# Seven-product weight blocks: low parts by adding transfers in place of VectorE subtractions

## The chip, the cores and the metric

One Trainium2 chip, one core. The metric is the device time of one execution in microseconds (us). The kernel before took 2408.53 us, the median of three runs (2404.02, 2408.53 and 2409.84).

## What is computed

One layer of a decoder trunk on a sequence of 1024 tokens with 1024 channels, all in float32. The part that this case touches is the wide dense products:

```python
u = x * (1.0 + scale1) + shift1
hq, hf, hi, hg, rq, rk, rv, rg, ga, gb = jnp.split(u @ w_in[l], split_at, axis=-1)
...
u = x * (1.0 + scale2) + shift2
h = jnp.square(jax.nn.relu(u @ w_up[l] + b_up[l]))
y = h @ w_down[l] + b_down[l]
```

Between them stand two recurrences (a gated linear one with 8 heads and a retention with 4), their output projections, and two LayerNorms. They stay as they are.

## The kernel before

**Three matmuls for one.** A float32 product is made of three passes in a rounded float32 format (F32R). Each operand is split into a high part, which is the operand rounded to that format, and a low part, which is the operand minus the high part. `mm3` (lines 164 to 168) then issues high x high, high x low and low x high. `split` (160 to 162) makes the two parts: a copy on ScalarE (ACT) writes the high part, a subtraction on VectorE (DVE) writes the low part.

**Seven products for eight.** For most wide projections the 2 x 2 block product is computed with seven block products (a scheme in the manner of Strassen and Winograd). A *group* is 256 columns of a weight matrix: 24 groups of `w_in` early in the program (4 of hg, 4 of ga, 8 of rg, and rq and rk four times each), and 15 groups of `w_up` late in it. For a group, `specs_S` (201 to 234) lists seven weight blocks of 128 partitions x 4 x 128: A11, A12 and A22 are cut straight from the loaded weights (tiles `raw`), S1, S2, S3 and S4 are sums and differences made on DVE (tiles `s`, line 212). In rq and rk the columns of a cut alternate between even and odd, so that neighbouring elements of such a block lie two apart in memory; elsewhere each partition has four runs of 128 elements. `seven` (365 to 397) goes through the groups; `product` (351 to 355) issues the twelve matmuls of one block product into a PSUM bank. The order within a group is A11, S1, S2, S4, S3, then A12 of the next group, then A22. The right-hand operands (tiles `U`: B11 to B22, T1 to T4) are split before the groups begin, by `combine` and `combos` (319 to 349).

**When blocks are made.** `W(..., ahead=4)` (297 to 307) calls `_split_to` (268 to 295), so that the split of the block for product n+4 is written in the program ahead of product n. The parts lie in the tiles `bh` (high) and `bl` (low), six buffers of each. So a block's split can start when the product six places ahead of it has read its buffer for the last time, and five products run from there to its own use. Raw weights have four buffers of 512 KB, two for each group; SyncE's queue (SP) issues their loads. The tiles `e` (12 buffers in the first stretch of groups, 14 in the second) carry the results: copies of banks (line 362), sums (374), gates (582 to 585), rotations (601 to 608) or squared ReLUs (1227, 1228). GpSimd's queue (POOL) writes results to memory: `hg_d`, `ga_d`, `rg_d`, `rq_d`, `rk_d` in the first stretch, `h_d` in the second. Every engine runs its own instructions strictly in the order that a scheduler gave them when the program was built.

Of the kernel before, what the change touches and what calls it, by code (L numbers as in the profile page):

```python
# [9 lines left out]
F32 = mybir.dt.float32  # L10
# [3 lines left out]
AF = mybir.ActivationFunctionType  # L14
ALU = mybir.AluOpType
# [104 lines left out]
class Trunk:  # L120
# [39 lines left out]
    def split(self, hi, lo, src):  # L160
        self.nc.scalar.activation(hi, src, AF.Copy)  # L161
        self.nc.vector.tensor_tensor(lo, src, hi.bitcast(F32), op=ALU.subtract)  # L162

    def mm3(self, out, wh, wl, uh, ul, start, stop, more=False):
        mm = self.nc.tensor.matmul
        r = mm(out, wh, uh, start=start, stop=False, skip_group_check=more)  # L166
        mm(out, wh, ul, start=False, stop=False, skip_group_check=more)  # L167
        return r, mm(out, wl, uh, start=False, stop=stop, skip_group_check=more)  # L168
# [99 lines left out]
    def _split_to(self, n):  # L268
        while self.w_split < min(n, len(self.w_tiles)):
            phase, key, place, ops, ids = self.w_tiles[self.w_split]  # L270
            if phase > self.w_phase:
                return
            self._load_to(max(ids) + 3)
            raws = [self.w_raw[i] for i in ids]
            if place == "raw":
                self.w_done[self.w_split] = raws
                self.w_split += 1
                continue
            if place == "s":
                hi = self.sp.tile([P, 4, P], F32R, tag="bh", bufs=6, name=self.uid("bh"))  # L280
                lo = self.sp.tile([P, 4, P], F32R, tag="bl", bufs=6, name=self.uid("bl"))
                self.split(hi, lo, ops(raws))
                self.w_done[self.w_split] = (hi, lo)
                self.w_split += 1
                continue
            if place == "U":
                t = self.ut(k=2)
                hi, lo = t[:, 0], t[:, 1]
            else:
                hi = self.wp.tile([P, 1024], F32R, tag="wh", bufs=3, name=self.uid("wh"))  # L290
                lo = self.wp.tile([P, 1024], F32R, tag="wl", bufs=3, name=self.uid("wl"))
            for d, i, s in ops:
                self.split(d(hi), d(lo), s(raws[i]))
            self.w_done[self.w_split] = (hi, lo)
            self.w_split += 1
# [1289 lines left out]
```

## Time and profile before

| | |
|---|---|
| time, median of three runs | 2408.53 us |
| the profiled execution's own time | 2413.24 us |
| its span | 2411.4 us |
| TensorE (PE) busy | 2324.8 us, 96% |
| VectorE (DVE) busy | 1633.0 us, 68% |
| ScalarE (ACT) busy | 950.7 us, 39% |
| GpSimd (POOL) busy | 256.3 us, 11% |
| moved by DMA | 326.28 MB, 135 GB/s on the mean |

Times in a profile are microseconds from the start of the span, "mean ns" is the mean of one instruction. Matmuls overlap: a matmul of 128 x 512 shows some 390 ns, while the next begins 0.23 us after it. "PE psa L166 <- ACT bh L161" reads: a matmul at line 166 into bank psa waited, and what ended the wait was ACT writing bh at line 161. In the rows of the timeline, the bracket gives the idle time ahead of an instruction and what ended it. In the stretches table, each engine has its busy time and, in brackets, its count of instructions; then follow the granted clock of TensorE, the share of time that the 16 DMA engines were busy (transfers that overlap on one engine count twice, so that it can pass 1), and the rate.

### The profile page before, as it was taken

Reading aid. Unit: us, or ns where it says so; the run is one execution under the profiler, and the core shown is the slowest. Engines: PE = TensorE matmul, PEld = TensorE weight load, DVE = VectorE, ACT = ScalarE, POOL = GpSimd, SP = SyncE. Lnnn points to the kernel's source line nnn. Section 1 sums busy time; section 2 is a strip of 40 time slices with the busy share of each in tenths; the row PEclk is TensorE's granted clock in tenths of the full one; section 3 lists DMA queues with packets and bytes.
Section 4 is the critical chain, followed back from the end, with each engine's and each line's share of the span. In section 5 each row is a group of like instructions: output and inputs, shape, how many; then the busy total and the mean of one; then the engine's idle time right before and its main releaser. Section 6 shows DMA issues by size and latency. Waiting matters only on the chain. (4 is left out here: it accounts for less than half of the span.)

```text
span 2411.4 us, 32875 instructions
## 1 busy us (share of the span) xinstructions
PE 2324.8 (96%) x12158; PEld 1980.6 (82%) x12158; DVE 1633.0 (68%) x3134; ACT 950.7 (39%) x1697; POOL 256.3 (11%) x396
## 2 busy tenths in 40 slices
PE   6999999999999999989999999999989999999997
PEld 5888888888988888889999877777778888788886
DVE  7997677673576777777666522468796666657668
ACT  4555333333232222244444412223465555644440
POOL 0111011010000000101101110004111112100001
PEclk9999999999999999999999998999999999999998
DMA  9433233332011111144334354348324444777653
GB/s 269 142 111 112 101 114 109 118 118 88 27 62 62 36 53 66 53 158 149 114 106 141 105 180 152 114 159 282 129 95 170 153 144 152 251 269 239 218 167 123
DMA packets 209857, 326.28 MB, mean 135 GB/s; under 512 B 14760, under 2 KB 136352, under 8 KB 209440
## 3 DMA queue, kind: packets, MB, share of 16 engines
q1 hardware_dynamic: 184784, 242.96, 31.3%
q0 software_dynamic: 24592, 80.77, 9.0%
q8 instruction: 96, 1.57, 0.3%
q14 instruction: 65, 0.53, 0.1%
q10 hardware_dynamic: 320, 0.45, 0.1%
HBM read 239.17 MB, written 84.94 MB: 134 GB/s over the span
## 5 line engine op out<-in xcount | busy, mean ns | idle before, releaser
L166 PE MATMUL psd<-U,wh 128*128 128x512 f32 x760 | 304.3, 408 | 19.2 <-ACT U L161 19.1
L167 PE MATMUL psd<-U,wh 128*128 128x512 f32 x760 | 304.3, 403 | 2.6 <-DVE U L162 2.5
L168 PE MATMUL psd<-U,wl 128*128 128x512 f32 x760 | 304.0, 402 | 1.4 <-DVE wl L162 1.4
L166 PE MATMUL psd<-U,bh 128*128 128x512 f32 x624 | 243.7, 391 | 2.7 <-DVE e L374 2.7
L168 PE MATMUL psd<-U,bl 128*128 128x512 f32 x624 | 243.5, 390 | 0.0
L167 PE MATMUL psd<-U,bh 128*128 128x512 f32 x624 | 243.4, 390 | 0.0
L166 PE MATMUL psd<-wh,U 128*128 128x256 f32 x768 | 222.0, 289 | 0.0
L167 PE MATMUL psd<-wl,U 128*128 128x256 f32 x768 | 219.5, 286 | 0.0
L168 PE MATMUL psd<-wh,U 128*128 128x256 f32 x768 | 218.9, 285 | 0.0
L166 PEld LDWEIGHTS psd<-U,wh 128*128 128x128 f32 x760 | 143.9, 191 | 56.0 <-ACT U L161 28.8
L161 ACT ACTIVATE wh<-raw 128x512 fp32r<-128x512 f32 (+1 forms) x110 | 85.8, 800 | 232.9 <-PE psd L167 202.9
L167 PEld LDWEIGHTS psd<-U,wh 128*128 128x128 f32 x760 | 146.1, 192 | 33.6 <-DVE U L162 6.3
L168 PEld LDWEIGHTS psd<-U,wl 128*128 128x128 f32 x760 | 146.2, 192 | 31.3 <-DVE wl L162 2.3
L161 ACT ACTIVATE bh<-s 128x512 fp32r<-128x512 f32 x156 | 98.5, 632 | 177.9 <-PE psd L167 77.8
L162 DVE TENSOR_TENSOR wl<-raw,wh 128x512 fp32r<-128x512 f32 (+1 forms) x110 | 98.0, 907 | 85.2 <-ACT wh L161 79.8
L166 PEld LDWEIGHTS psd<-wh,U 128*128 128x128 f32 x768 | 147.4, 192 | 2.7 <-issue 2.6
L167 PEld LDWEIGHTS psd<-wl,U 128*128 128x128 f32 x768 | 147.4, 192 | 0.1
L168 PEld LDWEIGHTS psd<-wh,U 128*128 128x128 f32 x768 | 147.4, 192 | 0.0
L162 DVE TENSOR_TENSOR bl<-raw,bh 128x512 fp32r<-128x512 f32 x117 | 80.0, 690 | 94.3 <-ACT bh L161 94.3
L166 PEld LDWEIGHTS psd<-U,bh 128*128 128x128 f32 x624 | 117.7, 189 | 28.3 <-DVE e L374 4.0
L167 PEld LDWEIGHTS psd<-U,bh 128*128 128x128 f32 x624 | 117.6, 188 | 24.5
L168 PEld LDWEIGHTS psd<-U,bl 128*128 128x128 f32 x624 | 117.4, 188 | 24.6
(373 smaller groups left out, 5459.7 us busy)
## 6 DMA issues: line engine op xcount, KB each, us to landing
raw<-in_w_in SPq DMA_DIRECT2D x96, 512.0 KB, 3.8
raw<-in_w_down SPq DMA_DIRECT2D x48, 512.0 KB, 4.7
raw<-in_w_ada SPq DMA_DIRECT2D x32, 512.0 KB, 4.1
raw<-in_w_up SPq DMA_DIRECT2D x32, 512.0 KB, 3.9
raw<-in_w_pb SPq DMA_DIRECT2D x20, 512.0 KB, 5.1
adw<-in_w_ada SPq DMA_DIRECT2D x16, 512.0 KB, 6.1
rg_d<-e POOLq DMA_DIRECT2D x32, 256.0 KB, 2.3
or_d<-ot POOLq DMA_DIRECT2D x32, 256.0 KB, 3.1
```

The costliest lines, as they stand in the source:

```text
L161: self.nc.scalar.activation(hi, src, AF.Copy)
L162: self.nc.vector.tensor_tensor(lo, src, hi.bitcast(F32), op=ALU.subtract)
L166: r = mm(out, wh, uh, start=start, stop=False, skip_group_check=more)
L167: mm(out, wh, ul, start=False, stop=False, skip_group_check=more)
L168: return r, mm(out, wl, uh, start=False, stop=stop, skip_group_check=more)
```

## The change

A second way to split, `split_by_dma`, is added. It writes the high part as before, then lets ACT write the negated high part into the low part's tile, and then issues a transfer from GpSimd's queue that adds the block to what stands there: -high + block. `_split_to` uses it for the weight blocks of the seven-product groups, other than A11, A12 and A22 of rq and rk, which keep the subtraction. Operands, products, buffers and everything else stay.

```diff
+    def split_by_dma(self, hi, lo, src):
+        A = self.nc.scalar
+        A.activation(hi, src, AF.Copy)
+        A.activation(lo, hi.bitcast(F32), AF.Copy, scale=-1.0)
+        self.nc.gpsimd.dma_start(lo, src, accum_op=ALU.add)
...
             if place == "s":
                 hi = self.sp.tile([P, 4, P], F32R, tag="bh", bufs=6, name=self.uid("bh"))
                 lo = self.sp.tile([P, 4, P], F32R, tag="bl", bufs=6, name=self.uid("bl"))
-                self.split(hi, lo, ops(raws))
+                src = ops(raws)
+                (self.split if key[0] in ("rq", "rk") and key[-1][0] == "A" else self.split_by_dma)(hi, lo, src)
```

In the changed kernel the lines behind line 163 have numbers that are 7 higher, those behind line 282 are 8 higher: line 162 stays, 212 becomes 219, and the lines 167, 168 and 169 are the three instructions of `split_by_dma`.

The first place is GpSimd's queue within one group of `w_up` (the seventh, whose results go to `h_d7`), in the stretch that lasts from 1812 to 2095 us in the profile. `h_d` are its writes of results from the tiles `e`. Before:

```order
L1217 DMA h_d7L_178<-e_17634 128x512
L1217 DMA h_d7S_183<-e_17700 128x512
L1217 DMA h_d7L_180<-e_17721 128x512
L1217 DMA h_d7S_181<-e_17696 128x512
L1217 DMA h_d7S_182<-e_17726 128x512
L1217 DMA h_d7L_179<-e_17768 128x512
L1217 DMA h_d7S_184<-e_17772 128x512
```

And now; the rows of `bl` are the adding transfers, from `raw` for blocks cut straight from the weights, from `s` for sums:

```order
L1225 DMA h_d7L_178<-e_17826 128x512
L169 DMA bl_17875<-raw_17663 128x4x128
L169 DMA bl_17899<-s_17900 128x512
L169 DMA bl_17929<-s_17930 128x512
L1225 DMA h_d7S_183<-e_17895 128x512
L169 DMA bl_17948<-s_17949 128x512
L1225 DMA h_d7L_180<-e_17917 128x512
L1225 DMA h_d7S_181<-e_17891 128x512
L1225 DMA h_d7S_182<-e_17922 128x512
L169 DMA bl_17975<-s_17976 128x512
L169 DMA bl_18006<-raw_17834 128x4x128
L1225 DMA h_d7L_179<-e_17966 128x512
```

The seven writes of a group keep their order, and seven adding transfers stand between them.

The second place is DVE where the groups of `w_up` begin, at about 1796 to 1803 us in the profile. `U` and `tf` belong to the splits of the right-hand operands T2, T3 and T4, `relu` to the first columns of `w_up`, and the first `s` is S1 of the first group. Before:

```order
L162 TENSOR_TENSOR U_16591<-U_16161,U_16590 128x1024 x2
L1241 TENSOR_TENSOR relu_16561<-relu_16526,relu_16468 128x512
L162 TENSOR_TENSOR U_16597<-tf_16581,U_16596 128x1024
L1246 TENSOR_TENSOR relu_16566<-relu_16497,relu_16561 128x512
L162 TENSOR_TENSOR U_16597<-tf_16581,U_16596 128x1024
L212 TENSOR_TENSOR s_16613<-raw_16282,raw_16284 128x512
L212 TENSOR_TENSOR s_16619<-s_16613,raw_16282 128x512
L162 TENSOR_TENSOR bl_16612<-s_16613,bh_16611 128x512
```

And now:

```order
L162 TENSOR_TENSOR U_16737<-U_16305,U_16736 128x1024
L219 TENSOR_TENSOR s_16759<-raw_16426,raw_16428 128x512
L162 TENSOR_TENSOR U_16743<-tf_16727,U_16742 128x1024
L1249 TENSOR_TENSOR relu_16707<-relu_16672,relu_16614 128x512
L162 TENSOR_TENSOR U_16743<-tf_16727,U_16742 128x1024
L1254 TENSOR_TENSOR relu_16712<-relu_16643,relu_16707 128x512
L219 TENSOR_TENSOR s_16766<-s_16759,raw_16426 128x512
L219 TENSOR_TENSOR s_16773<-raw_16428,s_16766 128x512
```

The first `s` now stands directly behind the split of T3, ahead of the split of T4 and of two subtractions of `relu`; the subtractions into `bl` are gone.

## The prediction

> **What bounds the kernel now.** The page comes first. PE is busy for nearly the whole span; the profiled execution took 2413.24 us, 1.8 us more than its span and 4.7 us more than the median of the runs, so I work out a difference and put it on the median, 2408.53.
>
> ```profile
> span 2411.4 us, 32875 instructions
> PE 2324.8 (96%) x12158; PEld 1980.6 (82%) x12158; DVE 1633.0 (68%) x3134; ACT 950.7 (39%) x1697; POOL 256.3 (11%) x396
> ```
>
> Shares over the whole span say little about the stretches that change, so the stretches table comes next: the 24 groups of w_in (76 to 540), the way into the second set of groups, and the 15 groups of w_up (1812 to 2095).
>
> ```profile
> core 0: us, PE busy (x) PEld busy (x) DVE busy (x) ACT busy (x) POOL busy (x), PEclk, DMA share, GB/s
> 76.00:540.00 464.00, 463.22 (x2042) 383.02 (x2041) 357.54 (x635) 198.74 (x329) 54.27 (x100) 1.00 0.35 117
> 1780.00:1812.00 32.00, 26.82 (x108) 21.60 (x107) 31.57 (x38) 21.21 (x31) 4.34 (x8) 0.89 0.31 105
> 1812.00:2095.00 283.00, 280.79 (x1232) 231.93 (x1231) 183.73 (x279) 170.98 (x284) 55.29 (x102) 0.99 0.49 169
> ```
>
> In both sets PE hardly ever rests. In the 32 us between them it does, and there DVE is busy 31.57 of 32. Third, PE's waits, first those from 76 to 540, then those from 1790 to 2100, complete:
>
> ```profile
> PE psa L166 <- ACT e L362: 0.6, 1, 0.6
> PE psd L166 <- DVE e L374: 0.2, 1, 0.2
> ```
>
> ```profile
> PE psa L166 <- ACT bh L161: 5.2, 1, 5.2
> PE psd L166 <- DVE e L374: 2.2, 1, 2.2
> ```
>
> So PE waited 8.2 us in all where the change acts, and 5.2 us of it is one wait. DVE, whose work is taken away, is not what holds up the groups. A gain can only come from that one wait; a loss can come from anything that makes PE wait where it doesn't now.
>
> **What is moved.** The groups of instructions have the prices.
>
> ```profile
> L162 DVE TENSOR_TENSOR bl<-s,bh 128x512 fp32r<-128x512 f32 x156 | 106.9, 686 | 44.3 <-ACT bh L161 44.2
> L161 ACT ACTIVATE bh<-s 128x512 fp32r<-128x512 f32 x156 | 98.5, 632 | 177.9 <-PE psd L167 77.8 <-PE psa L167 58.5 <-DVE e L603 16.7
> L162 DVE TENSOR_TENSOR bl<-raw,bh 128x512 fp32r<-128x512 f32 x117 | 80.0, 690 | 94.3 <-ACT bh L161 94.3
> ```
>
> Of 156 + 117 = 273 blocks, 8 x 3 keep the subtraction, so 249 change: 144 in the first set, 15 x 7 = 105 in the second. DVE loses 156 x 0.686 + 93 x 0.690 = 171 us, of which the waits above let PE see nothing but a part of the 5.2. ACT gains 249 negations; the nearest row is its copy of the same shape, 0.632 us, so 157 us. In the second set ACT goes from 171.0 to 171.0 + 105 x 0.632 = 237 us of 283, or 84%; it stays under PE. GpSimd gains 249 issues. What an adding transfer costs the trace doesn't show; its bounds are the plain ones, of 128 runs and of 512 runs:
>
> ```profile
> L585 POOL DMA_DIRECT2D rg_d<-e x32: 540/542/545, 268.3 to 548.8; - x32
> L1037 POOL DMA_DIRECT2D or_d<-ot x32: 750/783/831, 1094.2 to 1377.0; - x32
> ```
>
> At 0.54 to 0.83 us, GpSimd in the second set reaches 55.3 + 57 to 87, at most 142 us of 283.
>
> **The landing.** This is the unknown price. A block is 256 KB, within the core's memory.
>
> ```profile
> rg_d<-e POOLq DMA_DIRECT2D x32, 256.0 KB, 2.3
> or_d<-ot POOLq DMA_DIRECT2D x32, 256.0 KB, 3.1
> raw<-in_w_in SPq DMA_DIRECT2D x96, 512.0 KB, 3.8
> DMA to landing us min/median/max: 2.3/2.3/6.3
> ```
>
> The low end is 2.3 us, a plain write of that size from the same queue; the last row is of the same rg_d, with 6.3 us once in 32, under load, as the high end. I take 3.0, near or_d with its short runs and below a load of twice the bytes.
>
> **Inside a set.** Here the lead decides. The first row is ACT making the high part of an A12, the second the matmul that first uses it; the other two are the starts of two successive products.
>
> ```profile
> 1879.53 0.63 ACT L161 ACTIVATE bh<-raw 128x512 fp32r<-128x512 f32 x1 [2.09 <-PE psd L167]
> ```
>
> ```profile
> 1893.16 0.39 PE L166 MATMUL psc<-U,bh 128*128 128x512 f32 x1
> ```
>
> ```profile
> 1792.79 0.39 PE L166 MATMUL psc<-U,bh 128*128 128x512 f32 x1
> ...
> 1795.51 0.39 PE L166 MATMUL psd<-U,bh 128*128 128x512 f32 x1
> ```
>
> A product takes 2.72 us, and 1893.16 - 1879.53 = 13.63 is five of them, as the six buffers say. The low part has to be there for the third matmul, 0.45 us later. Copy and negation take 1.26 us. GpSimd may stand at a write of results: by the order, S4's transfer stands behind the write of the results' difference S3. The trace has that difference (first row) and the copy of S4's block (second):
>
> ```profile
> 1892.84 0.69 DVE L1235 TENSOR_TENSOR e<-e,e 128x512 f32<-128x512 f32 x1
> ```
>
> ```profile
> 1893.13 0.63 ACT L161 ACTIVATE bh<-s 128x512 fp32r<-128x512 f32 x1 [0.32 <-PE psd L167]
> ```
>
> The difference is there at 1893.5, the negation would end at 1894.4, so the write doesn't hold the transfer up. I allow 0.6 us for ACT's own queue. That leaves 13.6 + 0.45 - 1.3 - 0.6 = about 12 us for a landing of 2.3 to 6.3. The adding transfer brings a wait of GpSimd for ACT's negation; behind it stand the writes of `e`, which wait for later products in any case, and behind these the return of `e` buffers. A `raw` buffer is freed by the landing instead of DVE, some 3 us later, while its successor is needed two groups (38 us) on. Inside a set I put the change at nothing, hidden by five products of matmuls; without that cover each block would cost 1.3 + 3.0 us.
>
> **The way into the second set.** This is where a block is made just in time.
>
> ```profile
> 1782.66 1.29 DVE L162 TENSOR_TENSOR bl<-raw,bh 128x512 fp32r<-128x512 f32 x2
> ...
> 1798.69 0.69 DVE L1241 TENSOR_TENSOR relu<-relu,relu 128x512 f32<-128x512 f32 x1
> ...
> 1802.17 0.69 DVE L212 TENSOR_TENSOR s<-raw,raw 128x512 f32<-128x512 f32 x1
> ```
>
> ```profile
> 1796.00 1.99 ACT L161 ACTIVATE U<-tf 128x1024 fp32r<-128x1024 f32 x2
> 1802.89 1.36 ACT L161 ACTIVATE bh<-s 128x512 fp32r<-128x512 f32 x2 [4.90 <-DVE s L212]
> ```
>
> ```profile
> 1803.57 0.79 PE L166 MATMUL psa<-U,bh 128*128 128x512 f32 x1 [5.18 <-ACT bh L161]
> ...
> 1804.59 0.63 PE L168 MATMUL psa<-U,bl 128*128 128x512 f32 x1
> ```
>
> PE waits for S1, whose sum DVE makes at 1802.17. Two things bring that forward: the two subtractions of 1.29 us fall out of a DVE that works without a gap, and by the order the sum now stands behind the split of T3, where the row of 1798.69 was. One of the `relu` sums holds DVE for a moment, so I put S1's sum at 1797.6 to 1798.2 (1798.69 less 1.1). ACT is done with T4 at 1798.0: copy to 1798.8, negation to 1799.4, issue, and landed at 1799.4 + 3.0 = 1802.4. The third matmul can then run at 1802.4 where it ran at 1804.59: 2.2 us gained; with a landing of 2.3 us 2.9, with 6.3 a loss of 1.8. S2's sum follows the split of T4 at 1801.7, lands at about 1806.7, and PE, whose S1 product ends about then, loses nothing.
>
> **The way into the first set.** Here the cover is thinner than inside.
>
> ```profile
> 89.34 0.54 POOL L574 DMA_DIRECT2D gb_d<-gate  x1 [1.84 <-ACT gate L573]
> ```
>
> ```profile
> 89.88 1.15 ACT L161 ACTIVATE bh<-s 128x512 fp32r<-128x512 f32 x2
> ```
>
> ```profile
> 94.81 0.39 PE L168 MATMUL psd<-U,bl 128*128 128x512 f32 x1
> ```
>
> S2's and S4's copies run together from 89.88 and come ahead of both negations, so S2's ends at 91.6; GpSimd is past the gates' write (89.34) by then. Landed at 94.6 for a need at 94.81; some tenths more for the three negations ahead on ACT: I take 0.3 us lost, between 0 and 3.1 (landing of 6.3).
>
> **Sum.** Inside 0, second start -2.2, first start +0.3: -1.9 us, from -2.9 to +4.9. On the median: 2406.6, say 2407 us. About 0.3%, or 7.2 us, is what a measurement of this kernel can tell from no change, so the forecast is no difference.
>
> **Rivals.** *The DMA engines fill up in the second set.* An addition has to read two operands for each result. The most that the trace shows the engines move is in the load of the start:
>
> ```profile
> 40.00:50.00 10.00, 7.59 (x30) 5.60 (x28) 7.28 (x21) 4.80 (x8) 0.53 (x1) 0.83 1.10 341
> ```
>
> The second set moves 169 GB/s. Its 105 blocks are 27.5 MB, over 283 us 97 GB/s; counted once that is 266, counted twice 364. Above 341 the set stretches: 364/341 x 283 - 283 = 19 us, so 2407 + 19 = 2426. It decides from the point where a transfer costs the engines (341 - 169)/97 = 1.8 times its bytes. The first set stays below even then: 144 blocks, 37.7 MB over 464 us, 81 GB/s, twice makes 117 + 163 = 280. For it speaks that both operands must be read; against it, that 341 was met with loads from memory and need not be the limit, and that reads and writes may overlap. Chance 0.20. The Trainium skill says it of the chip: in "Collectives: The Full Stack", section "The bandwidth ceiling: the fold count and why AG ≠ RS ≠ AR", a reducing step is slower than a copying one, not through the addition but because each piece puts two reads on the same ring, with half the rate. By that rule the time would be the 2426 of this rival, where the row of plain writes gives 2407; no run here shows an adding transfer yet.
>
> *A block lands later than 12 us*, through an addition that is far slower than a copy or many short runs. Then five products take landing + 1.9 us: at 15 us 3.4 in place of 2.72 for each of 249 blocks, 0.66 x 249 = 164 us, so 2570. No row comes near; but no row shows an addition. Chance 0.06.
>
> *The second start gets free.* PE also ran slowly after its wait:
>
> ```profile
> 1804.00:1809.00 5.00, 5.00 (x13) 3.82 (x13) 5.00 (x9) 3.93 (x8) 0.00 (x0) 0.52 0.31 88
> ```
>
> At a clock of 0.52 the twelve matmuls to 1809 took some 2.4 us more than a usual product. If the shorter wait keeps the clock up and S1 lands at once, the wait's 5.2 and these 2.4 go: 2408.5 - 7.6 = 2401. But S1 still needs DVE, ACT and a landing. Chance 0.07. That the change does less than it says is excluded by the order: all 249 subtractions are gone and as many transfers stand there.
>
> **How the numbers follow.** Forecast 0.67, the rivals 0.20, 0.06 and 0.07. Faster by over 0.3% is the last, 0.07; slower the first two, 0.26; no difference 0.67. The range reaches from the free start, 2401, to the full engines and a little queueing, 2428; outside are late landings, an addition above twice its bytes, and little else, together under 0.2.
>
> **What would show it.** Right: subtractions of bl from s gone, 249 adding transfers landing in 2.3 to 6 us, ACT in the second set near 237 us, PE without a wait for bl inside either set, and a wait for bl of about 3 us near 1800. The second start fails if S1's transfer is issued after 1800.5 or lands after 1804. The first rival shows as a DMA share near 1 and 300 GB/s or more in the second set, with PE waiting for bl there; the second as landings above 12 us in both. The forecast is wrong if PE waits for transfers inside a set.

## The result, and the profile after

The changed kernel took 2519.27 us (median of four runs, 2516.97 to 2521.47) where the kernel before took 2408.22 (2404.02 to 2409.84): a ratio of 1.0464, with a 95% interval of 1.0446 to 1.0482. The forecast was 2407, in a range of 2401 to 2428. It was wrong by 112 us; the loss against the kernel before is 111.

The page of the changed kernel, first its head, then the row of GpSimd's transfers (packets, MB, share of the time of 16 DMA engines):

```profile
span 2519.6 us, 33500 instructions
PE 2358.7 (94%) x12158; PEld 1992.4 (79%) x12158; DVE 1477.9 (59%) x2885; ACT 1088.8 (43%) x1950; POOL 515.9 (20%) x645
...
q0 software_dynamic: 96160, 146.06, 27.3%
```

DVE lost 155 us of work, nearly the 171 that were reckoned, and ACT gained 138 (the negations' 155 less what other rows lost). The span grew by 108 us all the same. The last row prices the transfers: 27.3% of 2519.6 is 688 us, where the kernel before had 9.0% of 2411.4, 217 us; so, if the queue's other transfers cost what they did before, 249 adding transfers took 471 us of all sixteen engines, 1.89 us each. The transfers of that queue before, plain writes, took 217 us for 80.77 MB, 0.70 us for 256 KB.

The stretches, with the second one taken to where the second set now ends:

```profile
core 0: us, PE busy (x) PEld busy (x) DVE busy (x) ACT busy (x) POOL busy (x), PEclk, DMA share, GB/s
76.00:540.00 464.00, 434.12 (x1873) 352.63 (x1872) 252.56 (x463) 263.02 (x445) 184.43 (x225) 0.99 0.83 181
1830.00:2200.00 370.00, 323.54 (x1315) 258.13 (x1314) 138.83 (x203) 241.62 (x411) 171.71 (x212) 0.94 0.93 208
```

In the same 464 us of the first set PE runs 1873 matmuls where it ran 2042. In the second set it is busy for 87% of the stretch, at a lower clock, and the DMA engines are nearly always busy. The groups come more slowly. The difference S4 of the results is made once a group; its first and last start give the period, for before and then after:

```profile
L1246 DVE TENSOR_TENSOR e<-e,e x15: 684/693/693, 1824.3 to 2095.4; 128x512 f32<-128x512 f32 x15
```

```profile
L1254 DVE TENSOR_TENSOR e<-e,e x15: 683/684/694, 1877.8 to 2206.2; 128x512 f32<-128x512 f32 x15
```

That is 271.1 / 14 = 19.36 us a group before and 328.4 / 14 = 23.46 after; over 15 groups 61 us. The last write of `rg_d`, near the end of the first set, moved from 548.8 to 596.0, 47 us. Together they are the whole difference.

PE's waits after, from 76 to 560 and from 1790 to 2220 (of the second list the four longest):

```profile
PE psd L173 <- DVE e L382: 23.8, 12, 4.9
PE psa L173 <- ACT e L370: 4.8, 4, 2.2
PE psd L173 <- ACT e L370: 3.3, 1, 3.3
PE psd L175 <- DMA bl<-s: 0.3, 1, 0.3
```

```profile
PE psd L173 <- DVE e L382: 33.9, 13, 6.6
PE psa L173 <- ACT e L370: 6.2, 6, 4.4
PE psa L175 <- DMA bl<-s: 3.5, 1, 3.5
PE psd L175 <- DMA bl<-s: 1.4, 1, 1.4
...
```

Before, these stretches held 8.2 us of waits, now nearly 80. Almost none is for a low part (`bl`): the blocks do land in time. PE waits for DVE, which has less to do than ever, at line 382, the addition that empties a PSUM bank. What DVE waits for in turn, first in the first set, then in the second, and what SP's queue of loads waits for in the second:

```profile
DVE s L219 <- DMA bl<-s: 101.3, 46, 5.2
```

```profile
DVE s L219 <- DMA bl<-s: 109.5, 39, 5.8
```

```profile
SPq L272 <- DMA bl<-raw: 293.2, 29, 20.4
```

A sum `s` (line 219) waits until an adding transfer out of an older sum has landed. Loads of `raw` wait for transfers out of `raw`, where before they waited for DVE's subtractions; for such loads DVE waits 13.4 us in the second set and 14.3 in the first, so most of its waiting here is for the sums. One instance, engine by engine: GpSimd's issues, DVE, PE.

```profile
1980.03 0.87 POOL L169 DMA_DIRECT2D bl<-s  x1 [0.24 <-ACT bl L168]
1981.50 0.84 POOL L169 DMA_DIRECT2D bl<-s  x1 [0.59 <-ACT bl L168]
```

```profile
1986.14 0.69 DVE L219 TENSOR_TENSOR s<-raw,raw 128x512 f32<-128x512 f32 x1 [5.26 <-DMA bl<-s]
1986.75 0.68 DVE L1243 TENSOR_TENSOR e<-e,e 128x512 f32<-128x512 f32 x1
1987.35 0.68 DVE L382 TENSOR_TENSOR e<-psd,e 128x512 f32<-128x512 f32 x1
```

```profile
1988.09 0.50 PE L173 MATMUL psd<-U,bh 128*128 128x512 f32 x1 [2.56 <-DVE e L382]
...
1990.09 0.63 PE L173 MATMUL psd<-U,bh 128*128 128x512 f32 x1
1990.52 0.63 PE L174 MATMUL psd<-U,bh 128*128 128x512 f32 x1
```

The sum at 1986.14 takes the buffer of the sum four before it, which the first of the two transfers reads; it was released 6.1 us after that transfer's issue at 1980.03. DVE stood for 5.26 us with nothing to do but that sum, which nobody needed yet; behind it in order stood the addition that PE needed. From some 0.8 us after the restart the matmuls start 0.43 us apart instead of 0.23, until 1992.5. The Trainium skill has this in "TensorE: Matmul & The Clock Gate", section "Part 1: The HAM clock gate (the "warmup" mystery)": 426.7 ns from start to start while the clock is held back, 215.7 at full rate; the slow rows agree, and the fast ones here, 0.227 us, lie some 5% above. The waits account for some 70 us of the loss. Over both sets, matmuls that start over 0.3 us apart without a wait take together some 33 us more than at 0.227 us apart, and some 4 in the kernel before; so slow matmuls account for about 29 of the remaining 38.

The prices, first of the issues and negations, then of the landings (medians over the whole run):

```profile
L169 POOL DMA_DIRECT2D bl<-s x156 | 137.0, 882 | 137.1 <-ACT bl L168 119.5
L168 ACT ACTIVATE bl<-bh 128x512 fp32r<-128x512 f32 x249 | 155.2, 627 | 4.0
L169 POOL DMA_DIRECT2D bl<-raw x93 | 122.5, 1329 | 135.9 <-ACT bl L168 91.8
```

```profile
bl<-s POOLq DMA_DIRECT2D x156, 256.0 KB, 4.3
bl<-raw POOLq DMA_DIRECT2D x93, 256.0 KB, 4.4
```

### The profile page after: what moved, and what is told of

It is laid out like the page before. It is cut to its first block, busy times and chain, and to the rows that moved or that the text cites. A ratio compares the mean times of both kernels' runs of the same rounds, so it can differ in the third digit from the quotient of the medians.

```text
span 2519.6 us, 33500 instructions
## 1 busy us (share of the span) xinstructions
PE 2358.7 (94%) x12158; PEld 1992.4 (79%) x12158; DVE 1477.9 (59%) x2885; ACT 1088.8 (43%) x1950; POOL 515.9 (20%) x645
## 3 DMA queue, kind: packets, MB, share of 16 engines
q0 software_dynamic: 96160, 146.06, 27.3%
## 5 line engine op out<-in xcount | busy, mean ns | idle before, releaser
L173 PE MATMUL psd<-U,bh 128*128 128x512 f32 x624 | 256.2, 411 | 65.5 <-DVE e L382 61.4
L175 PE MATMUL psd<-U,bl 128*128 128x512 f32 x624 | 252.0, 404 | 1.7 <-DMA bl<-s 1.7
L174 PE MATMUL psd<-U,bh 128*128 128x512 f32 x624 | 252.2, 404 | 0.0
L173 PEld LDWEIGHTS psd<-U,bh 128*128 128x128 f32 x624 | 122.8, 197 | 103.4 <-DVE e L382 72.4
L169 POOL DMA_DIRECT2D bl<-s x156 | 137.0, 882 | 137.1 <-ACT bl L168 119.5
L168 ACT ACTIVATE bl<-bh 128x512 fp32r<-128x512 f32 x249 | 155.2, 627 | 4.0
L169 POOL DMA_DIRECT2D bl<-raw x93 | 122.5, 1329 | 135.9 <-ACT bl L168 91.8
L175 PEld LDWEIGHTS psd<-U,bl 128*128 128x128 f32 x624 | 122.7, 197 | 29.5 <-DMA bl<-s 2.6
```

Source lines behind the costliest of these rows:

```text
L168: A.activation(lo, hi.bitcast(F32), AF.Copy, scale=-1.0)
L169: self.nc.gpsimd.dma_start(lo, src, accum_op=ALU.add)
```

## The experiments

Three theories stood at first. **A**, the held sum: a sum's buffer, which DVE's own subtraction used to free, is now free only when its transfer has landed, and DVE's next sum waits for that, ahead of the bank additions. **B**, full DMA engines. **C**, the added work in the queues of ACT and GpSimd. After the first four runs came **D**, the held sources: not the sums alone but `raw` as well is held until a landing. In the table, before is the kernel before on the same chip; its profile rows are all from one profile.

| run | us | before | ratio, 95% interval | us a group, second set |
|---|---|---|---|---|
| the change | 2519.3 | 2408.2 | 1.0464 (1.0446 to 1.0482) | 23.46 |
| more sum buffers | 2541.6 | 2411.0 | 1.0543 (1.0527 to 1.0558) | 24.51 |
| load alone | 2523.3 | 2411.0 | 1.0456 (1.0427 to 1.0485) | 24.06 |
| only raw by transfer | 2485.6 | 2411.0 | 1.0312 (1.0292 to 1.0333) | 23.11 |
| only sums by transfer | 2442.8 | 2411.0 | 1.0133 (1.0114 to 1.0152) | 20.59 |
| nothing held | 2419.6 | 2413.5 | 1.0025 (1.0015 to 1.0034) | 19.45 |
| nothing held, short runs | 2423.7 | 2413.5 | 1.0040 (1.0025 to 1.0056) | 19.54 |
| copy for addition | 2453.2 | 2413.5 | 1.0161 (1.0147 to 1.0175) | 20.92 |
| two blocks only | 2412.0 | 2413.5 | 0.9991 (0.9982 to 1.0000) | 19.34 |
| only raw, two sum buffers | 2413.0 | 2410.7 | 1.0005 (0.9989 to 1.0021) | 19.36 |
| the change, two sum buffers | 2533.6 | 2410.7 | 1.0511 (1.0493 to 1.0529) | 25.06 |
| only sums held | 2481.5 | 2410.7 | 1.0293 (1.0271 to 1.0316) | 22.68 |
| hold alone | 2415.8 | 2410.7 | 1.0016 (1.0005 to 1.0028) | 19.48 |

The last column is worked out as above, from the first and last S4 difference of 15.

**More buffers for the sums.**

```diff
-                t = self.sp.tile([P, 4, P], F32, tag="s", bufs=4, name=self.uid("s"))
+                t = self.sp.tile([P, 4, P], F32, tag="s", bufs=7 if self.w_phase < 3 else 5, name=self.uid("s"))
```

> The changed kernel with more buffers for the sums: seven in the first set, five in the second, instead of four. Theory A, the held sum: DVE's next sum waits until the transfer of the sum four before it has landed, and through DVE's, ACT's and GpSimd's queues this closes into a loop of 24.0 us a group in the second set. With five buffers the loop is worth 24.0 x 4/5 = 19.2 us a group, below the 20.0 that PE needs, so the second set goes back from 361 to about 300 us, the first from 508 to about 461, DVE's 211 us of waits for landings shrink below 40, and the time is about 2410, at most 2425. Theory B, full DMA engines: the transfers cost 1.89 us of all sixteen engines each, 198 us in the second set beside 139 us of the rest, so the set cannot take less than 337 us, whatever the buffers: 2446 to 2519. Theory C, the queues of ACT and GpSimd: no change, about 2519.

2541.6 us: all three were off, and A fell in the form that it had. DVE's waits in the second set:

```profile
DVE s L219 <- DMA raw<-in_w_up: 134.8, 12, 17.0
...
DVE s L219 <- DMA bl<-s: 26.6, 15, 12.6
```

The wait for an older sum shrank from 109.5 to 26.6 us, as A said; in its place the sums now wait for loads of `raw`, 11 us at a time.

**All the load, without the dependency on sums.** DVE subtracts as before; beside it runs the load of the change, into a tile that nobody reads. The second set has two buffers fewer for results to make room for it.

```diff
+    def load_alone(self, hi, lo, src, of_sum):
+        t = (self.sx or self.sp).tile([P, 4, P], F32R, tag="x", bufs=3, name=self.uid("x"))
+        self.nc.scalar.activation(t, hi.bitcast(F32), AF.Copy, scale=-1.0)
+        self.nc.gpsimd.dma_start(t, hi if of_sum else src, accum_op=ALU.add)
...
-            k.e_bufs = 14
+            k.e_bufs = 12
+            k.sx = k.pool("s3", "right", se)
```

> All the load of the change without its dependency: the low parts are made by subtraction on DVE as before; beside this ACT negates each high part into a scratch tile of three buffers, and a transfer adds to the scratch tile, which nobody reads, the raw block or, for a sum, the high part (the sum itself is free at once). The first blocks of the second set have none, and the second set has 12 instead of 14 buffers for results. Theory A: no one waits for a landing but the scratch tile's next use, so 2408 to 2420, with the second set near 300 us. Theory B: the engines are as full as in the change, second set 337 us or more, 2446 to 2519. Theory C: ACT is as full and GpSimd issues as much, so about 2519.

2523.3 us, the whole loss, with no sum held. That spoke for B and C, it seemed; but the blocks from `raw` were still read by their transfers here.

**Only raw, and only sums, by transfer.** The choice in `_split_to` is made by `key[-1][0]`, "A" for a block from `raw`, "S" for a sum.

> Only the 93 blocks taken straight from raw go by adding transfer; the 156 sums are subtracted on DVE as before. Theory A: no sum is held, so about 2408, within 5. Theory B: 45 transfers x 1.89 = 85 us in the second set beside 139 leave the engines room, so also about 2408; a loss in proportion to the number of transfers would be 93/249 x 111 = 41 us, 2450. Theory C: ACT has 37 per cent of the added work, GpSimd's dearest issues (1.33 us) all remain: 2440 or more.

> Only the 156 sums go by adding transfer (these include the sums of all groups); the blocks from raw are subtracted on DVE. Theory A: the loop through the four sums is all there; ACT and GpSimd have less in it, so most of the loss stays: 2470 to 2515. Theory B: 60 transfers in the second set at 1.89 are 113 us beside 139, 252 of 283, so the engines have room and there is little loss: 2408 to 2425. Theory C: 63 per cent of the added work, about 2475.

2485.6 and 2442.8. A and B had no loss for raw alone, and it cost 75 us; C fits that run and misses the other by 32. For the sums alone A was too high (2470 at least) and B too low (2425 at most). The stretch of the second set in the raw-only run has the DMA engines busy for only 0.68 of the time, so B does not explain it:

```profile
1850.00:2100.00 250.00, 220.21 (x895) 177.00 (x894) 107.26 (x164) 130.37 (x221) 80.31 (x105) 0.94 0.68 160
```

Its timeline shows what does, in order of time GpSimd, SP's queue, DVE and PE:

```profile
1986.40 1.32 POOL L169 DMA_DIRECT2D bl<-raw  x1 [0.23 <-issue]
```

```profile
1991.60 23.39 SPq L272 DMA_DIRECT2D raw<-in_w_up  x3
```

```profile
1996.58 0.69 DVE L219 TENSOR_TENSOR s<-raw,raw 128x512 f32<-128x512 f32 x1 [5.32 <-DMA raw<-in_w_up]
1997.18 0.68 DVE L382 TENSOR_TENSOR e<-psa,e 128x512 f32<-128x512 f32 x1
...
1999.93 0.68 DVE L382 TENSOR_TENSOR e<-psd,e 128x512 f32<-128x512 f32 x1
```

```profile
2000.67 0.50 PE L173 MATMUL psd<-U,bh 128*128 128x512 f32 x1 [2.42 <-DVE e L382]
```

The transfer out of an A22 is issued at 1986.40; only when it has landed, at 1991.60, does the load into that buffer start; it lands 5 us later, and the sum S1 made from it waits 5.32 us on DVE, with the bank additions behind it. The same places in the kernel before, DVE and SP:

```profile
1940.03 0.69 DVE L162 TENSOR_TENSOR bl<-raw,bh 128x512 fp32r<-128x512 f32 x1 [0.79 <-ACT bh L161]
...
1946.20 0.69 DVE L212 TENSOR_TENSOR s<-raw,raw 128x512 f32<-128x512 f32 x1
```

```profile
1940.76 0.37 SPq L265 DMA_DIRECT2D raw<-in_w_up  x1
```

There the load starts as the subtraction of A22 ends, and S1's sum comes 5.4 us after the load's issue, for a load that takes 3.9 us (median). That sum is not for the group in hand but for the next one. The order of DVE before shows it (`raw_3133` and `raw_3134` are the two pieces of one group, `s_3180` is its S1, `s_3147` the S1 of the group ahead of it):

```
2534 L162 TENSOR_TENSOR bl_3146_17866<-s_3147_17867,bh_3145_17865 128x512
2535 L212 TENSOR_TENSOR s_3180_18029<-raw_3133_17802,raw_3134_17804 128x512
2536 L374 TENSOR_TENSOR e_3143_17858<-psa_3132_17801,e_3140_17840 128x512
...
2552 L162 TENSOR_TENSOR bl_3179_18028<-s_3180_18029,bh_3178_18027 128x512
```

The order puts every sum right behind the instruction that frees a buffer for it, here a whole group (19 us) ahead of its own split in row 2552. It is made early for no one's benefit, and whatever delays it delays the bank addition behind it. With more buffers it is put earlier still: in the run with more sum buffers S1's sum stands ahead of the addition out of `psa`, behind which it stands in the change, and its wait for the load grew to 10.62 us at 1972. That is why the first experiment lost.

**Nothing held.** The two operands change places; the block is read by ACT alone. The low parts come out with the opposite sign, so this is an experiment and not a repair.

```diff
-        A.activation(lo, hi.bitcast(F32), AF.Copy, scale=-1.0)
-        self.nc.gpsimd.dma_start(lo, src, accum_op=ALU.add)
+        A.activation(lo, src, AF.Copy, scale=-1.0)
+        self.nc.gpsimd.dma_start(lo, hi, accum_op=ALU.add)
```

> The two operands of the transfer change places: ACT writes the negated block itself into the low part, and the transfer adds the high part to it. So the block in raw and the sum are free as soon as ACT has read them, some 1.3 us after they were before, and not when the transfer lands; ACT, GpSimd and the DMA engines keep their 249 operations, DVE has none. The low parts come out with the opposite sign. Theory D, the held sources: what costs the time is that the next load of raw (SP's queue waited 293 us for bl<-raw in the second set of the change) and the next sum wait for a landing; here neither does, so 2408 to 2420. Theory B, full engines: 105 transfers at the 1.55 us of the sums-only run are 163 us beside 139, 302 of the 300 us that the second set takes, so the engines are just full and PE waits: 2430 to 2480. Theory C, the queues of ACT and GpSimd: 2480 to 2519.

2419.6 us, a loss of 0.25%, as D said. The stretch of the second set:

```profile
1850.00:2100.00 250.00, 246.46 (x1085) 203.42 (x1084) 102.51 (x154) 191.57 (x335) 123.84 (x174) 1.00 1.01 257
```

The engines are full, with a share of 1.01 and 257 GB/s; ACT and GpSimd have all their added work; and PE runs 1085 matmuls in 250 us where it ran 1086 before. That rules out B and C as the cause of all but a few us: 249 negations, issues and additions cost 6 us when neither a sum nor a load waits for a landing.

**Nothing held, with short runs.** A block from `raw` goes in two transfers of 512-byte runs, since the change's form out of `raw` has such runs too.

```diff
+        for b in (0, 1) if short else ():
+            self.nc.gpsimd.dma_start(lo[:, b::2], hi[:, b::2], accum_op=ALU.add)
```

> As the run in which nothing is held, but a block from raw goes in two transfers of 512-byte runs, about as many runs as the change's one transfer out of the rows of raw; low parts again with the opposite sign. Theory D: nothing is held, so again 2408 to 2425. If instead it is the dearer form of these 93 transfers that made the run with raw alone 74 us slower: 2470 or more. GpSimd has 93 issues more, which theory C counts as at least 80 us of its queue.

2423.7: the dearer form is not the cause either. The row of GpSimd's transfers and the stretch of the second set:

```profile
q0 software_dynamic: 97648, 146.06, 27.3%
```

```profile
1850.00:2100.00 250.00, 245.61 (x1083) 202.72 (x1081) 101.19 (x151) 189.91 (x332) 183.02 (x211) 1.00 1.10 258
```

The transfers take the same share as in the change, 27.3%, in a shorter span, and GpSimd is busier there than in the change; the loss is 0.4% instead of 4.6%.

**A copy in place of the addition.** The sources are held as in the change. The low parts are then the blocks themselves: the kernel leaves the subtraction out.

```diff
-        self.nc.gpsimd.dma_start(lo, src, accum_op=ALU.add)
+        self.nc.gpsimd.dma_start(lo, src)
```

> The change's transfers copy instead of adding, with the same sources, so the low parts are the blocks themselves and the subtraction is left out. Shows the price of the addition: a copy should take 0.7 to 1.5 us of the sixteen engines where the adding transfer took 1.89, and land in 2.3 to 3.5 us where it took 4.4. Theory D: the sources are still held, some 1 to 2 us less each, so part of the loss goes: 2440 to 2490. Theory B: the engines are far from full: about 2410 to 2420. Theory C: unchanged, about 2515.

2453.2: landings of 3.2 us (sums) and 2.9 (raw) instead of 4.3 and 4.4 take away 71 of the 111 us. That fits a loss that hangs on how long a source is held. The copies also load the engines and GpSimd less, so this run alone doesn't show it; but B had 2420 at most and C about 2515. The transfers' share fell to 20.0% of 2453.7, so a copy took 1.10 us of the engines and the addition 1.89, 1.7 times as much. The Trainium skill, in "Collectives: The Full Stack", section "The bandwidth ceiling: the fold count and why AG ≠ RS ≠ AR", gives a reducing step of a ring half the rate of a copying one; these transfers, which are no ring, came out a little better than that.

**Raw alone again, with two buffers for the sums.** By the order, S1's sum then stands two products, 5.4 us, later.

```diff
-                t = self.sp.tile([P, 4, P], F32, tag="s", bufs=4, name=self.uid("s"))
+                t = self.sp.tile([P, 4, P], F32, tag="s", bufs=2, name=self.uid("s"))
```

> As the run with only the 93 blocks from raw by transfer (2485.6), but with two buffers for sums in place of four. By the order a sum stands behind the moment at which its buffer comes free, with four buffers a whole group ahead of its use, with two some 5.4 us later. Theory D, refined: the loss of that run was the S1 sum, made a group ahead, waiting 5.3 us a group for a load of raw that a transfer's landing held up, with the bank additions behind it on DVE; two products later the load is there, so 2410 to 2420. If the price of the 93 transfers or their queue were the cause, fewer buffers could not help: 2485 or more.

2413.0, no loss that can be measured, with the same 93 transfers that had cost 75 us. DVE's waits for loads in the second set, first with four buffers, then with two:

```profile
DVE s L219 <- DMA raw<-in_w_up: 70.0, 13, 7.4
```

```profile
DVE s L219 <- DMA raw<-in_w_up: 6.9, 3, 3.2
```

This is the plainest of the runs: for `raw`, all the loss is the place of a sum in DVE's order against the return of a buffer.

**The whole change with two buffers for the sums** (the same line in the changed kernel).

> The change with two buffers for sums in place of four. Theory D: the wait for the load of raw goes as in the run beside it, the wait of each sum for the landing of an earlier sum's transfer stays, so about what the sums alone cost, 2430 to 2470. Theory A as first put, a loop through the ring of sums whose length per group goes with one over the number of buffers: 24.0 x 4/2 = 48 us a group in the second set, over 2700.

2533.6: both were off. The wait for loads (13.4 us in the change) went, as D said, but the sums' own wait did not stay as it was:

```profile
DVE s L219 <- DMA bl<-s: 158.9, 45, 6.4
```

It grew from 109.5 to 158.9 us. With two buffers a sum waits for the landing of the sum only two before it. For blocks from `raw` fewer buffers help, for the sums they hurt.

**Only the sums held.** All 249 transfers, the operands of the 93 from `raw` exchanged as above.

```diff
+        A.activation(lo, hi.bitcast(F32) if of_sum else src, AF.Copy, scale=-1.0)
+        self.nc.gpsimd.dma_start(lo, src if of_sum else hi, accum_op=ALU.add)
```

> All 249 transfers; for the blocks from raw the operands change places (ACT negates the block itself, the transfer adds the high part), so raw is free early and only the sums are held as in the change. Low parts of those 93 blocks have the opposite sign. Theory D: what the sums alone cost, 2435 to 2455 (2442.8 was measured with 156 transfers). If the loss went with the number of transfers: about 2515.

2481.5, above what D expected and below a loss in proportion. The only difference from the run with nothing held, 0.25%, is that sums are read by their transfers, so the held sums cost 2.7% at the full load. With 156 transfers alone it was 1.3%. DVE's waits, first with sums alone, then here:

```profile
DVE s L219 <- DMA bl<-s: 78.9, 42, 3.6
```

```profile
DVE s L219 <- DMA bl<-s: 118.0, 41, 6.4
```

Each wait grew from 1.9 to 2.9 us, and the sums' landings from 3.4 to 3.9 (medians). So the other transfers do add to the loss, by making landings longer. That is the part that B has in it. The two holds also don't add up: sums alone held cost 71 us, `raw` alone held (the run of load alone, which also keeps DVE's subtractions and has fewer buffers for results) 112, both together 111. An explanation would be that DVE waits only for whichever comes last; no run takes that apart.

**The hold alone.** The kernel before, and for each of the 93 blocks a transfer of 32 KB out of `raw`.

```diff
+        t = self.sp.tile([P, 64], F32, tag="x", bufs=4, name=self.uid("x"))
+        self.nc.scalar.activation(t, hi[:, 0, :64].bitcast(F32), AF.Copy, scale=-1.0)
+        self.nc.gpsimd.dma_start(t, src[:, 0, :64], accum_op=ALU.add)
```

> The kernel before, all subtractions on DVE, and beside them for each of the 93 blocks from raw a small adding transfer of 32 KB out of the block into a scratch tile that nobody reads, issued behind a short negation on ACT: hardly any load, but raw is free only when it has landed. Theory D: the load of raw starts some 3 to 4 us later in each group; about 1.6 us of that had no effect in the raw-only run, so 1 to 2 us a group are lost in the second set and less in the first: 2420 to 2440. Theories B and C: nothing, 2408 to 2414.

2415.8, less than D expected. The small transfers land in 2.2 us, and the sums' wait is there but short:

```profile
DVE s L225 <- DMA raw<-in_w_up: 23.7, 13, 2.5
```

1.8 us each, which costs 0.12 us a group; 70.0 / 13 = 5.4 each cost 23.11 - 19.36 = 3.75. By these two runs some 1.7 us of each wait are covered and the rest is lost; they don't show that this holds for other lengths.

**Two blocks only.** The kernel before with adding transfers for A12 and A11 of the first group of w_up, to look at the second start by itself.

```diff
+                (self.split_by_dma if key[:2] == ("up", 1) and key[-1] in ("A12", "A11") else self.split)(hi, lo, src)
```

> The kernel before, with adding transfers for the first two blocks of the second set alone (A12 and A11 of w_up's group 1), whose two subtractions stood on DVE ahead of the sum for which PE waited 5.2 us. All theories: nothing is held for long, DVE's sum comes 1.3 us earlier at least, PE's wait falls from 5.2 to between 1.5 and 3.9 us, and the time is 1.3 to 5 us below before: about 2405 where before has 2408.5; hardly more than can be measured.

PE's waits at the second start:

```profile
PE psa L175 <- DVE bl L162: 2.7, 1, 2.7
...
PE psa L173 <- ACT bh L161: 0.5, 1, 0.5
```

3.2 us instead of 5.2, so 2.0 us gained there, and a ratio of 0.9991 (0.9982 to 1.0000): as expected, at the edge of what can be measured. No run was clearly faster than the kernel before.

## Why the prediction was wrong, point by point

**What bounds the kernel** was read rightly: PE, with 8.2 us of waits, so that a gain could hardly come and a loss could come from any new wait.

**Inside a set** is the step that failed. It put the change there at nothing, on two grounds. The first held: the low part is needed some 12 us after its transfer can start, landings were 4.3 to 4.4 us in the median (3.0 was taken, with bounds of 2.3 to 6.3; the longest was 10.2), and PE waited for a `bl` only at the starts, 0.3 us in the first set and 3.5 and 1.4 in the second. The second ground was the sentence that a `raw` buffer is freed some 3 us later "while its successor is needed two groups (38 us) on". That counted from the use by the blocks' splits. But DVE reads the successor for S1's sum 5.4 us after the load's issue, a group ahead of its split, and the landing pushed the load back by 5 to 6 us. The sums' own buffers, of which the change moves the release in the same way, were not looked at, and most of DVE's waits came from them: 109.5 + 101.3 us. The term that was put at nothing cost nearly the whole 111 us; in the run with nothing held the loss was 6. The wait that came is not on the path of the low parts at all: it is on the path back, from a transfer that reads a tile to whoever fills that tile next. So the prediction's own sign of being wrong, PE waiting for transfers inside a set, didn't show either: PE waited for DVE, and DVE for the transfers. What stood behind the waiting sum, the bank additions, was likewise not asked for DVE; it was asked for GpSimd alone.

**The second start** was to gain 2.2 us. The rows of the changed kernel, GpSimd and PE:

```profile
1848.80 0.88 POOL L169 DMA_DIRECT2D bl<-s  x1 [2.52 <-ACT bl L168]
```

```profile
1847.89 0.50 PE L173 MATMUL psa<-U,bh 128*128 128x512 f32 x1 [0.49 <-ACT bh L167]
...
1852.16 0.57 PE L175 MATMUL psa<-U,bl 128*128 128x512 f32 x1 [3.54 <-DMA bl<-s]
```

S1's sum came early enough, as reckoned (PE waited 0.5 us for its high part where it had waited 5.2), and PE had the low part 3.4 us after its transfer's issue. PE waited 0.5 + 3.5 = 4.0 us instead of 5.2; but then 1.4 us more for S2's low part, which was to cost nothing. So about nothing was gained. (The prediction's loss of 1.8 us for a landing of 6.3 is a slip: by its own rows it is 1805.7 - 1804.59 = 1.1.)

**The first start** was to lose 0.3 us, at most 3.1, through a low part that lands late. PE waited 0.3 us for that, as reckoned. But first it waited 3.3 us for ACT's copy of a bank, which stood behind four negations in ACT's order. That wait was not in the prediction, which asked of the negations only how they delay the landing; with it the start lost 3.6 us, more than the bound.

**The rivals.** The first foresaw full engines, and they did fill: an adding transfer cost 2.7 times its bytes (1.89 against 0.70 us), past the 1.8 given as the point of decision, and the share went to 0.93 and above. But the run with nothing held shows that full engines cost 6 us (10 with short runs) as long as nobody but the products waits for the landings; this rival had the right sign and the wrong mechanism. Its measure was off too: at a share of 1.01 the engines moved 257 GB/s, well below the 341 that it took as their ceiling. Landings above 12 us never came. The second start did not get free.

## What to carry to other kernels

When a transfer takes over the work of an engine, ask not only when its result is needed but when its source is released: the tile that it reads stays taken until the landing, and the next writer of that tile may stand far earlier in an in-order queue than the use of what it writes. Read from the order where the next writer stands and what stands behind it; a buffer count that looks ample for the consumers says nothing of that. More buffers can make it worse where the scheduler moves the producer ahead as soon as a buffer comes free; freeing the source early removed the wait here, and so did a later place for the producer where only `raw` was held.

## What was not expected of the hardware

- An adding transfer of 256 KB inside the core's memory took 1.89 us of all sixteen engines in the change, 1.55 with sources in 128 long runs (18.8% of 2440.6 less 217, over 156), 2.50 with sources in runs of 512 bytes (18.1% of 2481.3 less 217, over 93). All three are estimates, since the 217 us of the queue's other transfers are taken from the kernel before. GpSimd spent 0.88 us on the issue of the one and 1.33 on that of the other, where plain writes took 0.54.
- With nothing held and the engines at a share of 1.01 (1850 to 2100 us), landings took 5.1 us in the median and 8.9 at most, where at a share of 0.82 in the first set the median was 3.6; 257 GB/s were moved. So full engines do lengthen landings, but inside the second set PE, with its lead of some 12 us, never waited for one: it ran 1085 matmuls in that stretch, 1086 before.
- A wait of PE of 2.56 us was followed, some 0.8 us after the restart, by 3.4 us of matmuls at a granted clock of 0.51 (1988.9 to 1992.3), so that over the whole kernel a wait cost some 40% more than its length (29 us on 70). Here is the stretch behind the wait at 1988:

```profile
1988.00:1993.00 5.00, 4.91 (x14) 3.88 (x15) 2.71 (x5) 3.04 (x5) 3.75 (x6) 0.66 0.76 220
```
